# Two of the four weight sums of each seven-product set formed by adding transfers instead of VectorE

## The chip, the cores and the metric

The kernel runs on one core of a Trainium2 chip. TensorE (PE in the profile) multiplies matrices, VectorE (DVE) and ScalarE (ACT) work on elements, GpSimd (POOL) has a small part, and SyncE (SP) issues almost all transfers between the device memory (HBM) and the on-chip memory (SBUF). Each engine takes its instructions in the order in which the program lists them; an engine that waits holds up everything listed behind the wait. The metric is the device time of one execution in microseconds (us). Lower is better.

## The reference

One decoder layer over 512 tokens of width 1024, in float32, batch 1. The two feed-forward blocks, which the change touches, are

```
mod = silu(c) @ w_ada + b_ada                    # nine vectors of 1024: shift, scale, gate, three times
u = rmsnorm(h) * g * (1 + sc) + sh
a, b = split(u @ w_in, 2)                        # w_in: 1024 x 5632, so a and b: 512 x 2816
h = h + 0.5 * gt * ((silu(a) * b) @ w_out)       # w_out: 2816 x 1024
```

The first block runs before, the second after a token-mixing block (a pooling mixer and a dilated window attention, gated and merged), which the change leaves alone. A last RMSNorm ends the layer.

## The kernel before

Activations are kept transposed, features on the 128 partitions and the 512 tokens along the free axis, so each product has a 128x128 block of a weight as the stationary operand and tokens as the moving one. To keep float32 accuracy each operand is split in two parts, hi and lo, and every product is three matmuls: hi*hi, hi*lo, lo*hi.

**The weight stream.** `plan` (L144) writes out by hand one list of *loads* (chunks of at most 128 x 1024 numbers, 512 KB) and one list `order` of *units*, the 128 x 1024 weight pieces in the sequence in which TensorE uses them. For each unit, `split_hi` (L271) has ScalarE copy the piece, rounded, into a ring `whi` (L294), and `split_lo` (L300) has VectorE store the rest into the ring `wlo` (L306). The rings hold about seven units. `look(n)` (L315) is called before each piece of TensorE work; it first lets `fetch` (L215) issue every load for which a buffer is free, then splits units up to n places ahead of the one about to be used (n is 4 around the code that changes, 3 in `ffn_tile`). A buffer comes free when the last unit that reads it has been split, which `self.last` records; the list of free buffers has three entries (`raw`, L1353) and two more (`rawx`, named X in the trace) from the first seven-product set of each feed-forward block on.

**Seven products in place of eight.** Most of `w_in` is used in sets of four column tiles (two gate tiles and two up tiles, `duo`, L723). Rows of `w_in` and tokens are cut in halves, and a two-by-two block product is done with seven block products instead of eight, in Winograd's manner. It needs sums of blocks of u, made once per feed-forward block by `u_steps` (L673), and sums of the weight blocks r11, r12, r22, r21, made for each set. I call one run of `duo` a *set*; there are seven sets in the first feed-forward block and nine in the second. `blocks` (L166) lists a set's seven units, u0 to u6:

```
u0 = r11              u1: x0 = r12 - r11    u2: x1 = r22 - x0    u3 = r21
u4: r12 = r22 - r12   u5 = r22              u6: x0 = r21 - x1
```

The four differences are made by VectorE in `make` (L234, the instruction is L240), each one 128 x 1024 subtraction. A make is issued just ahead of the split of its unit, or right after the ScalarE copy of the unit before it when its load has been issued.

**Around the products.** In `duo` (L754 to L777) each of the seven products is 24 matmuls of 256 columns (`product`, L712, lines L719 to L721). The products accumulate in three PSUM banks A, B, C; their order is A, B, A, C, A, B, A. After product 0 ScalarE copies A to C (`copy(C, A)`, L726 in the trace as bank<-bank), after product 1 B to p5, and so on; the next product on the same bank can't start before the copy has read it. `look(4)` before product 0 lists the split of u4, so the ScalarE copy of u4 stands ahead of `copy(C, A)` in ScalarE's order:

```
self.look(4)
self.product(bank, u, start)
self.step()
if i == 0:
    copy(C, A)
```

**The queue of SyncE.** `fetch` issues loads on SP (L224). In the first feed-forward block the same queue also carries the 512 KB pieces of `w_ada` for the nine vectors (`ada_fetch`, L348, L352), two of them in flight into the buffers `cs` and `AR`. `bg` (L379) has VectorE reduce such a piece (`ada_do`, L355, L360), and then lists the load of the next one into the same buffer, which must wait for that reduction. `ffn_pair` (L662) runs `bg` after each of its two tiles, so between the `look` of its second tile and the `look` before the next set's product 0 there is one such load.

Of the kernel before, what the change touches and what calls it, by code (L numbers as in the profile page):

```python
# [14 lines left out]
P = 128  # L15
# [121 lines left out]
class Kernel:  # L137
# [6 lines left out]
    def plan(self):  # L144
        (i1, o1), mix, (i2, o2) = chunk_widths()
        self.chunks = []
        for name, ws in (("wf1i", i1), ("wf1o", o1), ("wmix", mix), ("wf2i", i2), ("wf2o", o2)):
            off, rec = 0, []
            for w in ws:
                rec.append((name, off, w))  # L150
                off += P * w
            self.chunks.append(rec)
        f1i, f1o, mx, f2i, f2o = self.chunks


        self.loads, self.order, self.last = [], [], {}
        self.shifted = set()

        def plain(recs):
            for r in recs:  # L160
                n = len(self.loads)
                self.loads.append(r)
                self.last[n] = len(self.order)
                self.order.append((r[2], n, ("raw", n), None))

        def blocks(recs):  # L166
            n = len(self.loads)
            self.shifted.update(range(len(self.order), len(self.order) + 7))
            self.loads.extend(recs)
            r11, r12, r22, r21 = (("raw", n + i) for i in range(4))  # L170
            x0, x1 = ("x", 0), ("x", 1)
            for need, src, make in ((0, r11, None), (1, x0, (x0, r12, r11)), (2, x1, (x1, r22, x0)), (3, r21, None),
                                    (3, r12, (r12, r22, r12)), (3, r22, None), (3, x0, (x0, r21, x1))):
                for j, x in enumerate((r11, r12, r22, r21)):
                    if x == src or (make and x in make):
                        self.last[n + j] = len(self.order)
                self.order.append((D, n + need, src, make))

        def shift(i):

            self.shifted.update(range(len(self.order) - i, len(self.order)))

        def ffn(n, ins, outs, first):
            j, at = first, 0
            if first:
                plain(ins[:KT])
                at = KT
            for part, (k0, k1) in enumerate(PARTS):
                while j < pairs_before(n, part):
                    if j < PLAIN[n]:  # L190
                        plain(ins[at:at + 2])
                        if n and j < 2:
                            shift(2)
                        j, at = j + 1, at + 2
                    else:
                        blocks(ins[at:at + 4])
                        j, at = j + 2, at + 4
                plain(outs[part * KT // 2:(part + 1) * KT // 2] if part + 1 < len(PARTS) else outs[-KT:])

        ffn(0, f1i, f1o, FIRST)  # L200
        shift(3)
        base = len(self.order)
        plain(mx)
        self.shifted.update(range(base, base + 4))
        shift(2)
        ffn(2, f2i, f2o, 0)
        shift(4)
        self.fetched = self.done = self.made = 0
        self.pos, self.held, self.retired, self.half = 0, None, [], None
        self.at, self.start, self.top = {}, {}, 0  # L210
        self.buf = {}
        self.units = {base + i: 2 * P for i in (4, 5)}
        self.units.update({base + i: T for i in range(16, 20)})

    def fetch(self, n=None):  # L215

        n = len(self.order) - 1 if n is None else min(n, len(self.order) - 1)
        while self.fetched <= self.order[n][1] and self.free:
            i = self.fetched
            name, off, w = self.loads[i]  # L220
            src = self.a[name][off:off + P * w].rearrange("(p n) -> p n", p=P)
            self.buf[i] = self.free.pop(0)
            for c in self.pieces(i, w):
                self.nc.sync.dma_start(self.buf[i][:, c], src[:, c])  # L224
            self.fetched += 1

    def pieces(self, i, w):
# [6 lines left out]
    def make(self, i):  # L234

        while self.made <= i:
            m = self.order[self.made][3]
            if m:
                out, x, y = (self.source(z) for z in m)
                self.nc.vector.tensor_tensor(out, x, y, op=OP.subtract)  # L240
            self.made += 1

    def unit(self, i):
# [429 lines left out]
    def u_steps(self, n):  # L673
# [18 lines left out]
        def whole(u, k):  # L692
# [2 lines left out]
            return lambda: v.tensor_tensor(u.rearrange("p (k t) -> p k t", k=4), hi, lo, op=OP.add)  # L695

        last = split(3, a12)
        return ([whole(a11, 0), whole(a12, 4)] if n else []) + [add(a22, a21, a22, OP.add), split(0, a22), add(a21, a11, a21, OP.subtract), split(2, a21),
                add(a11, a22, a11, OP.subtract), split(1, a11), add(a12, a12, a11, OP.subtract)], last

    def step(self):

# [20 lines left out]
    def duo(self, j, first, last):  # L723
# [30 lines left out]
        for i, (bank, u, start) in enumerate(((A, blk(lo4, T1), True), (B, S[0], True), (A, S[1], False),  # L754
                                              (C, blk(hi4, T1), False), (A, S[2], False), (B, S[3], False),
                                              (A, blk(hi4, T2), False))):
            if i == 6:
                v.tensor_tensor(q(c)[:, :, 1, :], r(u3), r(p5), op=OP.add)
            self.look(4)
            self.product(bank, u, start)  # L760
            self.step()
# [12 lines left out]
                copy(u3, A)  # L774
            elif i == 6:
                silu(1, A)
                v.tensor_tensor(q(c)[:, :, 0, :], r(B), r(u2), op=OP.add)  # L777
        if last:
            mult()
            high()  # L780
# [783 lines left out]
```

## Time and profile before

| | |
|---|---|
| median of 3 runs | 1017.11 us (1016.72 to 1018.24) |
| span of the profiled execution | 1018.4 us; no other time of that execution is recorded |
| PE busy | 1007.5 us, 99% |
| PE weight loads busy | 913.3 us, 90% |
| DVE busy | 756.1 us, 74% |
| ACT busy | 437.2 us, 43% |
| POOL busy | 26.2 us, 3%, in 30 instructions |
| HBM read | 135.82 MB |
| granted TensorE clock | 0.997 |

A row of the timeline gives the start in us, the duration in us, the engine, the source line, the operation and its operands by tile name, with the idle time before it and what ended that in brackets. SPq rows are transfers being issued; their length is that of the issue, not of the transfer. A busy share of 99% for PE says only that matmuls overlap; whether TensorE really lost time is seen from the distance between its instructions' starts.

### The profile page before, as it was taken

What the parts mean: (1) busy time and instruction counts of PE and PEld (TensorE: products, weight loads), DVE (VectorE), ACT (ScalarE), POOL (GpSimd) and SP (SyncE); (2) the same over time, 40 slices, a digit from 0 to 9 for tenths busy, and PEclk for the clock granted to TensorE, in tenths of its full rate; (3) what the DMA queues carried; (4) which work ended last, traced back from release to release, by engine and by line L of the source; (5) the groups of instructions that cost most, each with busy time, mean ns of one, the idle gap of its engine ahead of it and who ended that gap; (6) DMA issues with size and microseconds to landing.
All of it is one profiled execution on the core that took longest, in us unless ns stands there. A gap on an engine that the chain in (4) does not pass through costs nothing.

```text
span 1018.4 us, 15580 instructions
## 1 busy us (share of the span) xinstructions
PE 1007.5 (99%) x6364; PEld 913.3 (90%) x6364; DVE 756.1 (74%) x1112; ACT 437.2 (43%) x668; POOL 26.2 (3%) x30
## 2 busy tenths in 40 slices
PE   8999999999999999999999999999999999999997
PEld 7888898989999999889988888998899899998997
DVE  6979879889786776879447776577787776676764
ACT  5453352625444552233414323364366254352553
POOL 0000000000000000007100000000000000000001
PEclk9999999999999999999999999999999999999998
DMA  8856465455533413122154773312243234241312
GB/s 314 287 196 246 136 211 176 175 168 174 168 111 112 147 46 104 52 83 83 32 198 167 248 271 121 117 53 78 88 168 123 80 105 145 84 144 44 111 34 83
DMA packets 43114, 139.61 MB, mean 137 GB/s; under 512 B 4897, under 2 KB 8225, under 8 KB 43042
## 3 DMA queue, kind: packets, MB, share of 16 engines
q1 hardware_dynamic: 42354, 137.95, 40.8%
q8 instruction: 50, 0.82, 0.3%
q10 hardware_dynamic: 688, 0.66, 0.2%
q14 instruction: 22, 0.18, 0.1%
HBM read 135.82 MB, written 2.77 MB: 136 GB/s over the span
## 4 chain that ended last, share of the span: by engine, by line
PE 94%; DVE 4%; ACT 0%; issue 0%; DMA 0%; DVEq 0%; ACTq 0%
PE bank L337 17%; PE bank L338 17%; PE bank L339 17%; PE bank L719 10%; PE bank L721 10%; PE bank L720 10%; PE bank L1494 1%; PE bank L1496 1%; PE bank L1498 1%; PE bank L1090 1%; PE bank L1269 1%; PE bank L1423 1%; PE bank L1270 1%; PE bank L1271 1%; PE bank L1038 1%; DVE wlo L306 1%
## 5 line engine op out<-in xcount | busy, mean ns | idle before, releaser
L306 DVE TENSOR_TENSOR wlo<-raw,whi 128x1024 fp32r<-128x1024 f32 (+6 forms) x173 | 177.4, 1037 | 67.6 <-ACT whi L294 67.1
L294 ACT ACTIVATE whi<-raw 128x1024 fp32r<-128x1024 f32 (+6 forms) x173 | 152.3, 899 | 40.6 <-DVE raw L240 39.0
L337 PE MATMUL bank<-UH,whi 128*128 128x512 f32 (+1 forms) x432 | 158.3, 366 | 0.0
L338 PE MATMUL bank<-UL,whi 128*128 128x512 f32 (+1 forms) x432 | 154.2, 357 | 0.1
L339 PE MATMUL bank<-UH,wlo 128*128 128x512 f32 (+1 forms) x432 | 154.1, 357 | 0.0
L337 PE MATMUL bank<-HI,whi 128*128 128x512 f32 (+1 forms) x406 | 146.6, 361 | 0.0
L338 PE MATMUL bank<-HK,whi 128*128 128x512 f32 (+1 forms) x406 | 146.3, 360 | 0.0
L339 PE MATMUL bank<-HI,wlo 128*128 128x512 f32 (+1 forms) x406 | 146.2, 360 | 0.0
L721 PE MATMUL bank<-UH,wlo 128*128 128x256 f32 x512 | 141.6, 277 | 0.0
L719 PE MATMUL bank<-UH,whi 128*128 128x256 f32 x512 | 141.6, 277 | 0.0
L720 PE MATMUL bank<-UL,whi 128*128 128x256 f32 x512 | 141.6, 277 | 0.0
L306 DVE TENSOR_TENSOR wlo<-X,whi 128x1024 fp32r<-128x1024 f32 (+4 forms) x96 | 105.3, 1103 | 39.0 <-ACT whi L294 38.7
L719 PE MATMUL bank<-SH,whi 128*128 128x256 f32 x384 | 107.1, 279 | 0.1
L720 PE MATMUL bank<-SL,whi 128*128 128x256 f32 x384 | 107.0, 279 | 0.0
L721 PE MATMUL bank<-SH,wlo 128*128 128x256 f32 x384 | 106.9, 278 | 0.0
L294 ACT ACTIVATE whi<-X 128x1024 fp32r<-128x1024 f32 (+4 forms) x96 | 89.9, 958 | 32.1 <-DVE X L240 28.9
L720 PEld LDWEIGHTS bank<-UL,whi 128*128 128x128 f32 x512 | 96.3, 188 | 0.3
L719 PEld LDWEIGHTS bank<-UH,whi 128*128 128x128 f32 x512 | 96.1, 188 | 0.3
L721 PEld LDWEIGHTS bank<-UH,wlo 128*128 128x128 f32 x512 | 96.1, 188 | 0.0
L339 PEld LDWEIGHTS bank<-UH,wlo 128*128 128x128 f32 x432 | 81.3, 188 | 12.1
L338 PEld LDWEIGHTS bank<-UL,whi 128*128 128x128 f32 x432 | 81.2, 188 | 11.7 <-issue 0.5
L337 PEld LDWEIGHTS bank<-UH,whi 128*128 128x128 f32 x432 | 81.2, 188 | 11.3 <-issue 0.5
(225 smaller groups left out, 1746.4 us busy)
## 6 DMA issues: line engine op xcount, KB each, us to landing
ada<-wada SPq DMA_DIRECT2D x47, 512.0 KB, 5.0
raw<-wmix SPq DMA_DIRECT2D x44, 512.0 KB, 3.6
raw<-wf1i SPq DMA_DIRECT2D x34, 512.0 KB, 4.3
raw<-wf2i SPq DMA_DIRECT2D x30, 512.0 KB, 3.5
X<-wf2i SPq DMA_DIRECT2D x14, 512.0 KB, 3.6
cs<-wada SPq DMA_DIRECT2D x12, 512.0 KB, 3.5
AR<-wada SPq DMA_DIRECT2D x12, 512.0 KB, 4.0
raw<-wf2o SPq DMA_DIRECT2D x12, 512.0 KB, 3.6
```

Of the source, the lines that this page charges most:

```text
L294: self.nc.scalar.activation(self.hi[:, y], r[:, x], AF.Copy)
L306: self.nc.vector.tensor_tensor(self.lo[:, y], r[:, x], self.hi[:, y], op=OP.subtract)
L337: M(ps, hi, uh, start=start, stop=False)
L338: M(ps, hi, ul, start=False, stop=False)
L339: M(ps, lo, uh, start=False, stop=stop)
L719: M(o, hi, uh, start=start and p == 0 and k == 0, stop=False, skip_group_check=True)
L720: M(o, hi, ul, start=False, stop=False, skip_group_check=True)
L721: M(o, lo, uh, start=False, stop=k == 3, skip_group_check=True)
L1038: M(S[:, o + i * P:o + i * P + P], qz[:, (2 * i + h) * P:(2 * i + h + 1) * P], k[:, toks], start=True, stop=True)
L1090: M(o, pt[:, blk * P:blk * P + P], v, start=i == 0, stop=i == len(srcs) - 1)
L1269: M(b, self.UH[k][:, c::4], hi, start=k == 0, stop=False)
L1270: M(b, self.UH[k][:, c::4], lo, start=False, stop=False)
```

## The change

Each set now has five loads instead of four: w11, t1, w22, w21, t3. For t1 and t3 SP loads the block w12 as before, and then a second transfer, issued on GpSimd's queue with an adding operation, adds another block from HBM onto it in SBUF: t1 = w12 + w11 and t3 = w12 + w22. w12 is thus loaded twice, and w11 and w22 are each read a second time by the adding transfers. The units become

```
u0 = r11   u1 = t1   u2: x1 = t1 + r22   u3 = r21   u4 = t3   u5 = r22   u6: x0 = x1 + r21
```

so `make` has two sums per set left, now additions. Since t1 and x1, t3 and x0 differ in sign from what they replace, two of the sums of u in `u_steps` and the two combining steps of the results in `duo` change between add and subtract; they are the same number of instructions of the same shapes. The adding transfer has to wait until the load under it has landed. The buffers stay the same: three, and five from product 0 of a block's first set on. r11's buffer now comes free after the split of u0, and t1's after the split of u2.

```diff
         def blocks(recs):
             n = len(self.loads)
             self.shifted.update(range(len(self.order), len(self.order) + 7))
-            self.loads.extend(recs)
-            r11, r12, r22, r21 = (("raw", n + i) for i in range(4))
+            w11, w12, w22, w21 = recs
+            self.loads.extend((w11, w12 + w11[:2], w22, w21, w12 + w22[:2]))
+            r11, t1, r22, r21, t3 = (("raw", n + i) for i in range(5))
             x0, x1 = ("x", 0), ("x", 1)
-            for need, src, make in ((0, r11, None), (1, x0, (x0, r12, r11)), (2, x1, (x1, r22, x0)), (3, r21, None),
-                                    (3, r12, (r12, r22, r12)), (3, r22, None), (3, x0, (x0, r21, x1))):
-                for j, x in enumerate((r11, r12, r22, r21)):
+            for need, src, make in ((0, r11, None), (1, t1, None), (2, x1, (x1, t1, r22)), (3, r21, None),
+                                    (4, t3, None), (4, r22, None), (4, x0, (x0, x1, r21))):
+                for j, x in enumerate((r11, t1, r22, r21, t3)):
...
-            name, off, w = self.loads[i]
-            src = self.a[name][off:off + P * w].rearrange("(p n) -> p n", p=P)
+            name, off, w, *more = self.loads[i]
+            at = lambda name, off: self.a[name][off:off + P * w].rearrange("(p n) -> p n", p=P)
             self.buf[i] = self.free.pop(0)
             for c in self.pieces(i, w):
-                self.nc.sync.dma_start(self.buf[i][:, c], src[:, c])
+                self.nc.sync.dma_start(self.buf[i][:, c], at(name, off)[:, c])
+            if more:
+                self.nc.gpsimd.dma_start(self.buf[i], at(*more), accum_op=OP.add)
...
-                self.nc.vector.tensor_tensor(out, x, y, op=OP.subtract)
+                self.nc.vector.tensor_tensor(out, x, y, op=OP.add)
...
-        return ([whole(a11, 0), whole(a12, 4)] if n else []) + [add(a22, a21, a22, OP.add), split(0, a22), add(a21, a11, a21, OP.subtract), split(2, a21),
-                add(a11, a22, a11, OP.subtract), split(1, a11), add(a12, a12, a11, OP.subtract)], last
+        return ([whole(a11, 0), whole(a12, 4)] if n else []) + [add(a22, a21, a22, OP.subtract), split(0, a22), add(a21, a11, a21, OP.subtract), split(2, a21),
+                add(a11, a22, a11, OP.subtract), split(1, a11), add(a12, a12, a11, OP.add)], last
...
-                v.tensor_tensor(q(c)[:, :, 1, :], r(u3), r(p5), op=OP.add)
+                v.tensor_tensor(q(c)[:, :, 1, :], r(p5), r(u3), op=OP.subtract)
...
-                v.tensor_tensor(q(c)[:, :, 0, :], r(B), r(u2), op=OP.add)
+                v.tensor_tensor(q(c)[:, :, 0, :], r(B), r(u2), op=OP.subtract)
```

## The prediction

> **What bounds the kernel now.** I read the page's busy times and its chain of waits first, then the table of stretches over the sets, then the timeline of each engine at the first set of a block.
>
> ```profile
> PE 1007.5 (99%) x6364; PEld 913.3 (90%) x6364; DVE 756.1 (74%) x1112; ACT 437.2 (43%) x668; POOL 26.2 (3%) x30
> ...
> PE 94%; DVE 4%; ACT 0%; issue 0%; DMA 0%; DVEq 0%; ACTq 0%
> ...
> 128.50:147.72 19.22, 19.22 (x169) 19.21 (x167) 15.68 (x17) 12.40 (x16) 0.00 (x0) 1.00 0.64 229
> 169.62:208.03 38.41, 38.41 (x337) 38.41 (x335) 33.06 (x36) 21.10 (x28) 0.00 (x0) 1.00 0.56 185
> 229.93:268.68 38.75, 38.70 (x336) 38.50 (x335) 34.42 (x41) 21.11 (x28) 0.00 (x0) 1.00 0.57 184
> 290.58:329.00 38.42, 38.42 (x337) 38.42 (x336) 27.86 (x29) 19.43 (x27) 0.00 (x0) 1.00 0.35 113
> sum 307.66, PE 307.61 PEld 307.38 DVE 239.53 ACT 165.68 POOL 0.00; mean PE 38.45 PEld 38.42 DVE 29.94 ACT 20.71 POOL 0.00
> ```
>
> TensorE holds 94% of the chain. The table's stretches are runs of sets; the columns are PE, PEld, DVE, ACT and POOL busy, then the granted clock, the DMA share and GB/s. The sum row covers all eight runs, sixteen sets: 307.66 us. One set takes 19.22 us, two take 38.42, whether DVE is busy 33.06 us of them or 27.86. The only run that is longer is the one from 229.93: 38.75 instead of 38.42, so 0.33 us lost. That is all that the sixteen sets lose to anything but TensorE's own pace, and it bounds what relief of DVE can bring there.
>
> **What is removed.** The next row is the table for L240 alone, over the whole span; below it is the chain inside the stretch where DVE falls behind.
>
> ```profile
> 0.00:1018.40 1018.40, 78.05 (x64) 1.00 0.41 137
> ...
> 213.80 1.22 DVE cs L360 x2
> ...
> 231.07 1.14 DVE X L240
> ...
> 238.49 1.15 DVE X L240
> 239.79 0.90 issue
> 240.69 0.58 ACT u L726
> 241.31 0.39 PE bank L719
> ```
>
> The 64 makes cost DVE 78.05 us; half go, so 39 us, all beside matmuls. From 213 to 240 us the chain runs through DVE, which has the `w_ada` reductions to do as well, and ends in the 0.33 us gap at 241.31. The make at 231.07 is u4's and goes (1.14 us); the one at 238.49 is u6's and stays. 1.14 is more than 0.33, so the gap closes: **-0.33 us**. What is late next there is TensorE itself. The changed signs are as many instructions of the same shapes: 0.
>
> **What is added.** Per set one more load on SP and two adding transfers on POOL's queue, 3 x 512 KB, for sixteen sets 25 MB on top of 135.8 MB. POOL has 0.00 us of work in the sets, so its queue is empty; the DMA share there is 0.34 to 0.64, and 7 transfers in 19.22 us instead of 4 fit if they are in time. So the cost is not volume but lateness: t1 and t3 are ready only after two transfers, one behind the other. I call A the time from the landing of the load under it to the landing of the adding transfer. The trace has no such transfer. Its nearest rows (KB each, median us from issue to landing), and the one measured duration of a POOL instruction that I use:
>
> ```profile
> raw<-wf1i SPq DMA_DIRECT2D x34, 512.0 KB, 4.3
> raw<-wf2i SPq DMA_DIRECT2D x30, 512.0 KB, 3.5
> ...
> scr<-q SPq DMA_DIRECT2D x1, 528.0 KB, 2.6
> v<-scr SPq DMA_DIRECT2D x1, 528.0 KB, 3.8
> ...
> L1157 POOL TENSOR_SCALAR k<-rt 64x496 f32<-64x496 f32 x4 | 6.0, 1510 | 0.3
> ```
>
> An adding transfer must fetch a block from HBM, read the block in SBUF and write it. From below, it is one plain load: A = 3.5. From above, two of the slower ones: A = 8.6, and 10.1 with a POOL instruction of 1.51 us ahead. I take the two streams that it is made of, one out of SBUF (2.6) and one into it (3.8): **A = 6.4**, an estimate that lies between the ends.
>
> The Trainium skill, DMA: Bandwidth & Descriptors, section Anatomy of one DMA — SWDGE (gpsimd) path, fits a transfer issued from GpSimd as 2.0 us plus its bytes at 436 GB/s, an estimate of 3.2 us for 512 KB, or 4.4 if the bytes count twice; with these the sum below would be 1019.3 or 1020.5. No run here shows a transfer of that queue yet.
>
> **Place 1: the first set of the first block.** Only three buffers exist before its product 0. By the code t3, the fifth load, takes t1's buffer, which is given back at the split of u2; the next `look` is the one before product 0. On SP that is behind the `w_ada` load that `bg` lists after the pair's second tile.
>
> ```profile
> 128.50 0.28 PE L719 MATMUL bank<-UH,whi 128*128 128x256 f32 x1
> ...
> 131.33 0.28 PE L719 MATMUL bank<-SH,whi 128*128 128x256 f32 x1
> ...
> 134.21 0.28 PE L719 MATMUL bank<-SH,whi 128*128 128x256 f32 x1
> ...
> 129.96 1.05 ACT L294 ACTIVATE whi<-raw 128x1024 fp32r<-128x1024 f32 x1
> 132.01 1.07 ACT L294 ACTIVATE whi<-raw 128x1024 fp32r<-128x1024 f32 x1 [1.00 <-DVE raw L240]
> 132.97 0.58 ACT L726 ACTIVATE bank<-bank 128x512 f32<-128x512 f32 x1
> ...
> 120.95 1.28 DVE L306 TENSOR_TENSOR wlo<-X,whi 128x256 fp32r<-128x256 f32 x2
> 124.84 1.23 DVE L306 TENSOR_TENSOR wlo<-X,whi 128x1024 fp32r<-128x1024 f32 x1 [1.46 <-ACT whi L294]
> 125.98 1.22 DVE L360 SCALAR_TENSOR_TENSOR AR<-AR,cond 128x1024 f32<-128x1024 f32 x1
> ...
> 123.41 0.33 SPq L352 DMA_DIRECT2D cs<-wada  x1
> 123.83 0.38 SPq L224 DMA_DIRECT2D raw<-wf1i  x1
> 127.24 0.33 SPq L352 DMA_DIRECT2D AR<-wada  x1
> ```
>
> Products 0, 1 and 2 start at 128.50, 131.33 and 134.21. u4's ScalarE copy runs at 132.01, behind its make; copy(C, A) follows and ends at 132.97 + 0.58 = 133.55. Product 2 adds to bank A and needs that copy, so u4's copy may start no later than 134.21 - (133.55 - 132.01) = 132.67. There is 0.66 us of room today.
>
> After: the `AR` load still goes out at 127.24, for it waits for the reduction at 125.98, which no removed make delays (the split ahead of it, at 124.84, waited 1.46 us for ACT). t3's load follows 0.42 later, as the load at 123.83 follows the one at 123.41: 127.66. It takes 4.3, lands at 131.96, and the sum is there at 131.96 + A. ACT stands at u4's copy until then, with copy(C, A) behind it, and TensorE at product 2. The stall is 131.96 + A - 132.67 = A - 0.71: **5.69 us** for 6.4. It is paid once: behind it ACT has 3.7 us of copies (three of 1.05, one of 0.58) for the 5.7 us until product 4 wants the next one, and DVE's split of u4, 1.22 us after ACT's, is wanted only two products later. u4's own make, which DVE drops, was not what TensorE waited for.
>
> **Place 2: the first set of the second block.** The same three buffers, no `w_ada` loads, but t3's buffer waits for t1 as a sum.
>
> ```profile
> 734.94 0.28 PE L719 MATMUL bank<-UH,whi 128*128 128x256 f32 x1
> ...
> 731.70 1.06 ACT L294 ACTIVATE whi<-raw 128x1024 fp32r<-128x1024 f32 x1 [5.00 <-DVE raw L240]
> 737.97 0.58 ACT L726 ACTIVATE bank<-bank 128x512 f32<-128x512 f32 x1 [5.20 <-PE bank L721]
> ...
> 715.23 0.33 SPq L224 DMA_DIRECT2D raw<-wf2i  x1
> ...
> DMA to landing us min/median/max: 4.4/4.4/4.4
> ```
>
> u4's copy runs at 731.70 and then ACT idles 5.20 us, so there is room. The deadline, by the spacings of place 1, is 734.94 + 5.71 - 1.54 = 739.11. t1 is the second load, issued at 715.23 and landing 4.4 later (the last row is that load's), at 719.6; as a sum at 719.6 + A. ACT's copy (1.05) and DVE's two reads of it (1.22 each, the first beside the copy) hold the buffer about 2.4 more; t3's load lands 3.5 later and is a sum A later: 725.5 + 2A. The stall is 2A - 13.6 where that is positive: 0 for 6.4 (12.8), hidden by 0.8 us; the cover is gone at A = 6.8.
>
> **The other fourteen sets** have five buffers. The tightest are the eight sets that follow another set directly, where t3 takes the buffer of the r21 before it.
>
> ```profile
> 760.71 0.33 SPq L224 DMA_DIRECT2D X<-wf2i  x1
> 761.09 0.42 SPq L224 DMA_DIRECT2D raw<-wf2o  x1
> ...
> DMA to landing us min/median/max: 3.5/3.5/4.5
> ...
> 776.39 0.58 ACT L726 ACTIVATE bank<-bank 128x512 f32<-128x512 f32 x1 [1.17 <-PE bank L721]
> ```
>
> t3's load would go where the one at 761.09 stands, behind r21's at 760.71; the slowest there took 4.5, so it lands at 765.6. The next set's copy(C, A) is at 776.39 and must end 2.88 us after product 0, near 779.2, so u4's copy may start at 777.6. Hidden up to A = 12. t1 has 7 units' time and is no tighter. Sets behind output tiles have more, since those units last twice as long. SP's order else only shifts by one load per set.
>
> **The sum**, against the span of 1018.4: + 5.69 + 0 - 0.33 = +5.4, so 1023.8. The median of the runs lies 1.3 under that span, so for the median 1017.1 + 5.4 = **1022.5**.
>
> **The rivals.**
> *The adding transfer is as short as a plain one* (A = 3.5): 2.79 - 0.33 = +2.5, 1019.6. For it: a 528 KB transfer out of SBUF lands in 2.6. Against: it has both to read and to write SBUF. The Trainium skill's fit named above would be this case.
> *It is long* (A from 6.8 to 12): both first sets stall. At 8.6: 7.89 + 3.6 - 0.33 = +11.2, 1028.3; at 10.1: 9.39 + 6.6 - 0.33 = +15.7, 1032.8. For it: nothing in the trace prices POOL's part of the issue.
> *It is so long that the steady sets stall* (A above 12). At 15: 14.3 + 16.4 + 8 x 3 - 0.33 = +54, 1071. Against: more than three times any 512 KB row.
> *Not slower: t3 is in time.* t1's buffer is physically free when DVE's split of u1 has read it, near 122.2 (the row at 120.95). If t3's load stood on SP before 122.0, not behind the `AR` load, it would land at 126.3 and be a sum by 132.7, and the stall at place 1 would vanish: -0.33, 1016.8. Against it is the order of the code: nothing fetches between the split of u2 and the `look` before product 0.
> *Faster by more than can be told apart*, if 39 us less DVE work helps TensorE in a way that the 0.33 us don't show. Nothing in the set table speaks for it: two sets with 5.2 us more DVE work than two others (33.06 and 27.86) last as long.
>
> **How the numbers follow.** Chances: place 1 alone with A from 4.4 to 6.8, 45%; short, 19%; long, 17%; steady sets stall, 6%; in time, 9%; faster, 4%. The time is that of the first. A median of these runs can be told from another at about 0.2%, 2.0 us. Slower then holds the first four but a hundredth of the short case, 86%; same 10%; faster 4%. The range runs from 1018.8 (A near 2.8) to 1032.7 (A = 10.1) and leaves out the steady stall, the in-time and the faster case and the edge of the short one, 2 in 10.
>
> **What the profile after would show.** 32 instructions at L240 and about 39 us less DVE; POOL's queue with 32 transfers; in the sets' table 38.4 for all pairs but a first set of 19.2 + 5.7 in the first block, with ACT's copy of u4 idle on a DMA just before copy(C, A), and t3's load issued just behind an `AR` load. The second block's first run stays at 57.6. I am wrong if the first set stays at 19.2 (the in-time rival), if the eight following sets grow, or if matmuls of the same shape are spaced differently.

## The result, and the profile after

The changed kernel takes 1042.92 us (median of 4 runs, 1040.52 to 1043.74), the kernel before on the same chip 1017.67 us (4 runs, 1016.72 to 1019.89). The ratio is 1.0241 with a 95% interval of 1.0221 to 1.0261. The forecast was 1022.5 us with a range up to 1032.7: the sign was right, the added time was nearly five times what was forecast. The profiled execution of the changed kernel took 1043.39 us, with a span of 1041.6 us.

From the page of the kernel after: busy times, the two large transfer queues, what was read, and the chain of waits by engine.

```profile
PE 1010.3 (97%) x6364; PEld 914.2 (88%) x6364; DVE 720.3 (69%) x1080; ACT 437.4 (42%) x668; POOL 54.3 (5%) x62
...
q1 hardware_dynamic: 44658, 146.34, 41.2%
q0 software_dynamic: 4608, 16.78, 9.2%
...
HBM read 160.98 MB, written 2.77 MB: 157 GB/s over the span
...
PE 80%; DMA 9%; DVE 6%; ACT 2%; issue 2%; SPq 0%; DVEq 0%; ACTq 0%; POOLq 0%
```

32 VectorE instructions and 35.8 us of VectorE work are gone, and 32 transfers stand on GpSimd's queue (q0). TensorE's share of the chain falls from 94% to 80%, and transfers, which held nothing, hold 9%.

The table of stretches of the kernel after, one row for each run of sets, from its first matmul to the first one behind it. The columns are PE, PEld, DVE, ACT and POOL busy, the granted clock, the DMA share and GB/s.

```profile
125.65:152.53 26.88, 21.74 (x170) 21.52 (x168) 14.71 (x15) 12.26 (x16) 1.73 (x2) 0.87 0.64 200
174.31:217.77 43.46, 39.36 (x337) 38.76 (x336) 31.60 (x37) 19.75 (x26) 2.60 (x3) 1.00 0.73 212
239.56:282.10 42.54, 39.73 (x337) 39.27 (x336) 31.84 (x38) 19.84 (x27) 2.36 (x3) 1.00 0.72 217
303.89:342.42 38.53, 38.53 (x338) 38.53 (x337) 25.13 (x27) 19.11 (x26) 0.86 (x1) 1.00 0.49 148
747.65:815.68 68.03, 60.05 (x505) 59.64 (x504) 42.30 (x43) 33.11 (x44) 5.20 (x6) 0.95 0.62 175
837.47:876.00 38.53, 38.53 (x338) 38.53 (x337) 25.68 (x26) 20.05 (x27) 1.74 (x2) 1.00 0.54 159
897.78:936.31 38.53, 38.53 (x338) 38.53 (x336) 25.68 (x26) 20.03 (x27) 1.74 (x2) 1.00 0.55 159
958.09:996.62 38.53, 38.53 (x337) 38.52 (x336) 24.61 (x26) 19.19 (x27) 0.88 (x1) 1.00 0.44 137
sum 335.03, PE 315.01 PEld 313.31 DVE 221.57 ACT 163.34 POOL 17.12; mean PE 39.38 PEld 39.16 DVE 27.70 ACT 20.42 POOL 2.14
```

With the same borders, the runs of the kernel before took 19.33, 38.52, 38.87, 38.53, 57.73, 38.53, 38.52 and 38.53 us, 308.56 in all. So the sets lost 26.5 us, in four runs of the eight: 7.5 in the first set, 4.9 and 3.7 in the next two runs, 10.3 in the second block's first run. 20.0 us of it are idle time of TensorE (335.03 - 315.01); the other 6.5 are matmuls that took longer. The stretches between the runs are as before, but for the start: the sets begin at 125.65 us instead of 128.50. That is no effect of the change: among the kernels below one without any adding transfer starts its sets at 125.69 (e5_dose), one with all of them at 128.74 (e4_early_fetch). It goes with the TensorE clock at the start. The trace before records full clock from 19.27 us on, e4_early_fetch from 19.86, the kernel after from 11.57 and e5_dose from 11.66; around 12 us eight matmuls of 128x1 take 1.71 us in the first two and 0.99 and 1.03 in the others. 26.5 less these 2.9 and 0.4 in stretches elsewhere is the 23.2 us between the two spans.

**Where it waits.** Rows of the timeline of the kernel after, queue by queue: first at the first set of the first block, then at the second run of sets, then in the second block's first run. Brackets give the idle time before the row and what ended it.

```profile
124.39 0.33 SPq L355 DMA_DIRECT2D AR<-wada  x1
124.81 0.38 SPq L225 DMA_DIRECT2D raw<-wf1i  x1
...
129.75 0.86 POOL L227 DMA_DIRECT2D raw<-wf1i  x1 [21.93 <-DVE wlo L309]
...
135.07 1.06 ACT L297 ACTIVATE whi<-raw 128x1024 fp32r<-128x1024 f32 x1 [6.91 <-DMA raw<-wf1i]
136.03 0.58 ACT L729 ACTIVATE bank<-bank 128x512 f32<-128x512 f32 x1
...
136.66 0.58 PE L722 MATMUL bank<-SH,whi 128*128 128x256 f32 x1 [5.14 <-ACT bank L729]
...
176.27 0.33 SPq L355 DMA_DIRECT2D AR<-wada  x1
176.70 0.37 SPq L225 DMA_DIRECT2D raw<-wf1i  x1
...
183.43 0.88 POOL L227 DMA_DIRECT2D raw<-wf1i  x1 [22.09 <-DMA raw<-wf1i]
...
192.50 1.06 ACT L297 ACTIVATE whi<-raw 128x1024 fp32r<-128x1024 f32 x1 [4.76 <-DMA raw<-wf1i]
193.46 0.58 ACT L729 ACTIVATE u<-bank 128x512 f32<-128x512 f32 x1
...
194.10 0.39 PE L722 MATMUL bank<-UH,whi 128*128 128x256 f32 x1 [2.01 <-ACT u L729]
...
757.31 0.81 SPq L225 DMA_DIRECT2D X<-wf2i  x2
...
763.03 0.86 POOL L227 DMA_DIRECT2D X<-wf2i  x1 [14.14 <-DMA X<-wf2i]
...
771.07 1.06 ACT L297 ACTIVATE whi<-X 128x1024 fp32r<-128x1024 f32 x1 [9.59 <-DMA X<-wf2i]
...
772.66 0.58 PE L722 MATMUL bank<-UH,whi 128*128 128x256 f32 x1 [6.45 <-ACT u L729]
```

The first place is the one forecast, link by link: t3's load 0.42 us behind the `AR` load, the adding transfer behind the landing of that load, ScalarE idle on it, copy(C, A) behind u4's copy, and TensorE idle for 5.14 us. The other two were not forecast. There it is t1 that is late, the second unit of a set that directly follows another. ScalarE reaches that unit while TensorE is still in the set ahead, and stands at it with the copy of bank A (L729, at 193.46) behind it; so the matmul that waits is the first of the last product of the set ahead. The adding transfer is issued at 183.43 and ScalarE starts on the sum at 192.50, 9.07 us later; at 763.03 and 771.07 it is 8.04 us. The first set of the second block lost 1.53 us on its own t3 (matmul at 755.05).

**The transfers.** The table for the adding line, L227, over the whole execution: durations of the issuing instruction (min/median/max in ns; one of four such rows), and the time from issue to landing of all 32.

```profile
L227 POOL DMA_DIRECT2D raw<-wf2i x12: 858/872/917, 733.1 to 970.2; - x12
...
DMA to landing us min/median/max: 5.1/6.7/9.2
```

**The clock.** Stretches of the kernel after around the first long stall; the column before the last two is the granted clock.

```profile
131.10:136.50 5.40, 0.42 (x4) 0.21 (x2) 0.34 (x1) 1.43 (x2) 0.00 (x0) 0.81 0.55 97
136.60:138.60 2.00, 1.94 (x9) 1.94 (x10) 1.77 (x2) 2.00 (x4) 0.00 (x0) 0.50 0.08 14
138.60:140.60 2.00, 2.00 (x11) 2.00 (x11) 2.00 (x3) 1.00 (x2) 0.00 (x0) 0.50 0.89 264
140.60:142.60 2.00, 2.00 (x17) 2.00 (x16) 1.72 (x2) 1.16 (x3) 0.00 (x0) 0.83 0.91 285
```

The clock falls to half while TensorE waits, and stays there for 6.83 us in the records, so the product behind the stall runs at half speed: 11 matmuls in 2 us in place of 17 and more. The first set lost 7.5 us: 5.3 is the delay at the stall (5.42 us from one matmul start to the next, where 0.12 is usual), the other 2.2 is this. The same happens behind the stall at 772.66.

### The profile page after: what moved, and what is told of

It is laid out like the page before. It is cut to its first block, busy times and chain, and to the rows that moved or that the text cites. A ratio compares the mean times of both kernels' runs of the same rounds, so it can differ in the third digit from the quotient of the medians.

```text
span 1041.6 us, 15684 instructions
## 1 busy us (share of the span) xinstructions
PE 1010.3 (97%) x6364; PEld 914.2 (88%) x6364; DVE 720.3 (69%) x1080; ACT 437.4 (42%) x668; POOL 54.3 (5%) x62
## 3 DMA queue, kind: packets, MB, share of 16 engines
q0 software_dynamic: 4608, 16.78, 9.2%
## 4 chain that ended last, share of the span: by engine, by line
PE 80%; DMA 9%; DVE 6%; ACT 2%; issue 2%; SPq 0%; DVEq 0%; ACTq 0%; POOLq 0%
PE bank L340 15%; PE bank L341 15%; PE bank L342 15%; PE bank L722 8%; PE bank L724 8%; PE bank L723 8%; DMA X<-wf1i 3%; DMA AR<-wada 2%; DVE wlo L309 2%; DMA raw<-wf2i 2%; PE bank L1497 1%; PE bank L1501 1%; PE bank L1499 1%; DMA X<-wf2i 1%; PE bank L1093 1%
## 5 line engine op out<-in xcount | busy, mean ns | idle before, releaser
L309 DVE TENSOR_TENSOR wlo<-raw,whi 128x1024 fp32r<-128x1024 f32 (+5 forms) x182 | 190.4, 1058 | 85.6 <-ACT whi L297 83.5
L297 ACT ACTIVATE whi<-raw 128x1024 fp32r<-128x1024 f32 (+5 forms) x182 | 163.8, 917 | 55.8 <-DMA raw<-wf1i 33.4
L309 DVE TENSOR_TENSOR wlo<-X,whi 128x1024 fp32r<-128x1024 f32 (+4 forms) x87 | 92.0, 1067 | 56.8 <-ACT whi L297 56.7
L297 ACT ACTIVATE whi<-X 128x1024 fp32r<-128x1024 f32 (+4 forms) x87 | 78.8, 928 | 36.4 <-DMA X<-wf1i 14.3
```

Of the source, the lines that this page charges most:

```text
L297: self.nc.scalar.activation(self.hi[:, y], r[:, x], AF.Copy)
L309: self.nc.vector.tensor_tensor(self.lo[:, y], r[:, x], self.hi[:, y], op=OP.subtract)
```

## The experiments

Times are medians of 4 runs (10 for e1_no_add and e7_hybrid), with the kernel before on the same chip: 1017.33 us beside e1 to e4 (but e3b), 1017.62 beside e5, e6, e7 and e10, 1017.01 beside e11 to e13, and 1017.35 beside e3b. A set's length is taken as in the table above, from the one profiled execution of each kernel. That is not always a typical one: those of e2_plain_pool and e3b_t1_only were the fastest of their four, 2.9 and 1.8 us under the median. A stall is given as the idle time before its row; where an expectation speaks of a hold, its number is the distance between two matmul starts, which is 0.28 us longer. Where an edit adds a line, the line numbers of its rows are one higher.

**No adding transfer (e1_no_add).** The kernel after without them; SP's five loads, the order and VectorE's two sums stay. t1 and t3 are then w12 alone, so all sums by transfer are left out.

```diff
-            if more:
-                self.nc.gpsimd.dma_start(self.buf[i], at(*more), accum_op=OP.add)
```

> The changed kernel without the 32 adding transfers (t1 and t3 are then w12 alone, so the sums are left out); the fifth load of each set, the new order of buffers and the two makes per set stay. Theory 1, the loss is the wait for sums that are late in a few sets: all sets run at 19.2 us and the time is that of before, 1016 to 1018. Rival, the fifth load and the changed order of buffers cost by themselves: 1025 or more stays.

Measured: 1017.15 us (1016.12 to 1020.03), ratio 1.0004 [0.9993, 1.0016]. All runs of sets are back at 19.33, 38.53 and 57.73 us, but the third, which took 39.18. So the loss needs the second transfers: the fifth load, SP's new order and the changed signs cost nothing but perhaps those 0.3 us, and 36 us less VectorE work bring nothing.

**The second transfer without the addition (e2_plain_pool).** It is issued on GpSimd's queue, with the same bytes, the same wait and the same place, but overwrites; so w12's part of the sums is left out.

```diff
-                self.nc.gpsimd.dma_start(self.buf[i], at(*more), accum_op=OP.add)
+                self.nc.gpsimd.dma_start(self.buf[i], at(*more))
```

> The second transfer of t1 and t3 is plain instead of adding, still on GpSimd's queue and still behind the landing of the load under it (the sums are left out). Theory 1a, half of the length of an adding transfer is the adding itself (its 4 KB packets take 328 ns, those of plain loads 159): the second transfer lands 1.6 to 3 us sooner, the first set stalls some 3.7 us instead of 5.3, runs two and three of the first block lose 2 us or less in place of 8.6, the second block's first run 3 to 4 in place of 10.3; about 1026. Rival 1b, two transfers in a row and GpSimd's way of issuing are the length: 1038 or more.

Measured: 1031.06 us (1028.2 to 1031.58), ratio 1.0131 [1.0116, 1.0147], between the two. The first set takes 24.97 us (5.6 more) and the second block's first run 62.85 (5.1 more), both with half clock for 3.41 us; the second and third run of the first block take 38.53, no loss at all. Landing takes 3.7/4.5/6.8 us (min/median/max) in place of 5.1/6.7/9.2. From the page of this kernel, the row of GpSimd's queue:

```profile
q0 software_dynamic: 4608, 16.78, 5.0%
```

As many packets and bytes as in the kernel after took 5.0% of 16 engines' span instead of 9.2%. Per packet that is 16 x 0.050 x 1026.4 / 4608 = 0.18 us, against 16 x 0.092 x 1041.6 / 4608 = 0.33: the addition nearly doubles the time that a packet holds a DMA engine. By the medians, 13.7 of the 25.3 us are the second transfer as such, behind the first, and the rest is the addition's; in the two profiled executions it is 10.4 of 26.5 in the sets.

**Only t3, only t1 (e3_t3_only, e3b_t1_only).** In the first, t1's adding transfers are left out (t1 = w12), in the second t3's.

```diff
-            self.loads.extend((w11, w12 + w11[:2], w22, w21, w12 + w22[:2]))
+            self.loads.extend((w11, w12, w22, w21, w12 + w22[:2]))
```
```diff
+            self.loads.extend((w11, w12 + w11[:2], w22, w21, w12))
```

> Adding transfers for t3 alone; t1 is w12 alone (its sum is left out). Theory 1 as read from the trace: t3 stalls the first set of the first block (5.3 us and 2.2 more at half clock, 7.5), t1 stalls runs two and three of that block (8.6) and the second set of the second block (6.6 and 1.8), and it makes t3 late in that block's first set (1.7). So 7.5 stay and the time is about 1025. Rival, t3 is the late one in runs two and three too: 1033 or more.

> The other half of the run with t3's sums alone: the sixteen adding transfers of t1 stay, those of t3 are left out, so that sum is missing in every set. If t1 is what holds the second and third run of the first block and the first run of the second (4.9, 3.7 and 10.3 us), and t3 what holds the first set, the first set is 19.3 us again, the three runs keep most of their 18.9 us, and the time is 1030 to 1036 us. Rival: t1 is late there only because both transfers of a set stand on GpSimd's queue and share the DMA engines; then the three runs lose most of what they lost, and the time is below 1026 us.

Measured: with t3 alone 1025.99 us (1024.48 to 1027.8), ratio 1.0093 [1.0076, 1.011]; with t1 alone 1023.15 us (1021.32 to 1024.02), ratio 1.0052 [1.0032, 1.0073]. The one run of sets that is longer with t3 alone, and then the one that clearly is with t1 alone, from the tables of stretches:

```profile
125.83:152.90 27.07, 21.78 (x170) 21.57 (x168) 14.71 (x15) 12.26 (x16) 1.00 (x1) 0.87 0.64 202
```
```profile
732.36:793.61 61.25, 58.22 (x505) 58.02 (x504) 41.76 (x43) 32.64 (x44) 2.58 (x3) 1.00 0.56 169
752.20:754.20 2.00, 2.00 (x17) 2.00 (x18) 1.84 (x2) 1.81 (x2) 0.00 (x0) 1.00 0.09 31
```

t3 alone costs the first set 7.7 us, and nothing in any other: all of place 1, and t3's transfers of the fifteen other sets are hidden, as forecast. t1 alone costs 3.5 us in the second block and 0.1 in the first. Together they make 11 us in the profiled sets, not 26.5 (by the medians 8.7 + 5.8 = 14.5, not 25.3). The second and third run of the first block lose only when both transfers are there, so the first account of e3b, that t1 by itself holds them, fell and its rival held. (The last row is the clock behind a stall of 3.03 us: full.)

**Loads listed earlier (e4_early_fetch).** `look` fetches once more after its splits, so that t3's load stands on SP ahead of the `w_ada` load. Nothing is left out.

```diff
         self.fetch()
         self.split(self.pos + ahead)
+        self.fetch()
```

> The changed kernel, complete, with one line more: look() issues loads again right after its splits, so that a load is listed on SP as soon as its buffer is given back and not behind the w_ada loads that come before the next look(). Theory 2, in the first block the place on SP behind w_ada loads makes the sums late: the first set's 7.5 and most of the 8.6 of runs two and three go, the second block keeps its 10.3; 1026 to 1029. Rival, the length of the adding transfer alone decides: 1038 or more.

Measured: 1041.1 us (1038.39 to 1044.52), ratio 1.0238 [1.0214, 1.0261]. The first set is nearly cured (21.12 us, 1.8 more, at full clock), so place 1 is the order on SP. The second and third run are no better, 43.79 and 46.58 us, so for them theory 2 fell. Rows of the second run: GpSimd's, SP's queue, then VectorE's.

```profile
172.18 0.87 POOL L227 DMA_DIRECT2D raw<-wf1i  x1 [13.60 <-DMA raw<-wf1i]
...
172.94 0.33 SPq L356 DMA_DIRECT2D AR<-wada  x1
...
180.89 1.22 DVE L364 SCALAR_TENSOR_TENSOR AR<-AR,cond 128x1024 f32<-128x1024 f32 x1 [4.37 <-DMA AR<-wada]
182.04 0.08 DVE L364 DVE_READ_ACCUMULATOR AR<-AR,cond 128x1 f32 x1
182.04 1.29 DVE L309 TENSOR_TENSOR wlo<-raw,whi 128x256 fp32r<-128x256 f32 x2
```

t1's adding transfer now goes out at 172.18, half a microsecond into the run and not nine as in the kernel after, and the `w_ada` load at 172.94 runs beside it: it lands at 180.86, after 7.9 us. VectorE stands at that piece's reduction for 4.37 us with the splits and makes of the set behind it. The wait has moved from t1 to the load beside its transfer.

**Without the `w_ada` loads, and both edits together (e6_no_ada_loads, e10_early_no_ada).** In the first block's sets the loads into `cs` and `AR` are left out after the first two; the second kernel has the earlier listing too.

```diff
-        for c in np.split(np.arange(D), n):
+        self.ring = getattr(self, "ring", 0) + (self.ada_free is not None)
+        for c in np.split(np.arange(D), n) if self.ring < 3 or self.ada_free is None else ():
```

> The changed kernel without the w_ada loads of the first block's sets, after the first two; the reductions stay and read old data, so that part of the computation is left out. Theory L (the second and third run of sets of the first block lose their 4.9 and 3.7 us to the w_ada loads, which stand on SP ahead of the load of the sums and share the transfers with it): both runs go back to 38.5 us, the first set keeps a part of its loss or none, the second block keeps its 10 us, and the time is 1027 to 1035 us. Rival (the sums themselves take too long there, or VectorE's reductions are what holds them): the two runs keep their losses and the time is about 1042 us.

> The last edit and the earlier listing of the loads together. If the losses of the first block are the listing (first set) and the w_ada loads (second and third run), nothing but the second block's 10 us and at most 2 us of the first set are left: 1027 to 1030 us. If the sums of the second and third run are late for another reason, their 5 and 8 us stay: about 1041 us.

Measured: 1025.68 us (1024.78 to 1027.68), ratio 1.0063 [1.0045, 1.008]; with both 1027.92 us (1026.39 to 1028.1), ratio 1.0079 [1.0064, 1.0094]. The first block loses nothing in the first kernel (19.32, 38.53, 38.53 and 38.53 us) and 0.4 in the second; the second block keeps 9.0 and 10.1. The second and third run without these loads:

```profile
166.10:204.63 38.53, 38.53 (x338) 38.53 (x336) 29.66 (x32) 20.31 (x26) 1.73 (x2) 1.00 0.56 158
226.41:264.94 38.53, 38.53 (x337) 38.52 (x336) 30.91 (x37) 19.95 (x27) 1.73 (x2) 1.00 0.54 156
```

So all 16 us of the first block hang on the `w_ada` loads, beside which the sums are made. The edit takes away their bytes and their places on SP together.

**Small `w_ada` loads (e13_small_ada).** This tells their bytes from their place: they stay on SP, but load 128 of 1024 columns.

```diff
-            c = slice(c[0], c[-1] + 1)
+            c = slice(c[0], c[-1] + 1 if self.ring < 3 or self.ada_free is None else c[0] + 128)
```

> The changed kernel with the w_ada loads of the first block's sets cut to their first 128 columns (an eighth of the bytes) after the first two, in the same places of SP's list, with whole reductions that read old data behind them; so part of that computation is left out. Theory O (the loss of the first block comes from the order on SP, where the load of a sum waits behind a w_ada load and through it for VectorE): the first block keeps most of its 16 us, and the time stays at 1037 us or more. Theory S (the loss comes from the transfers that w_ada's loads and the adding ones share, which makes both late): the first block loses what it lost without these loads, and the time is near 1026 us. In between, 1030 to 1036 us, both have a part.

Measured: 1034.88 us (1032.91 to 1035.87), ratio 1.0173 [1.0158, 1.0188]: both have a part, and the sets show which. The first three runs of sets, and then the landing times of the adding transfers in the first block, from 120 to 300 us (min/median/max):

```profile
127.07:153.15 26.08, 21.64 (x170) 21.43 (x168) 14.71 (x15) 12.27 (x16) 1.72 (x2) 0.93 0.64 197
174.93:213.46 38.53, 38.53 (x337) 38.52 (x336) 29.74 (x32) 20.09 (x26) 2.60 (x3) 1.00 0.68 192
235.25:274.40 39.15, 38.77 (x337) 38.57 (x336) 30.89 (x37) 19.97 (x27) 2.60 (x3) 1.00 0.64 189
```
```profile
DMA to landing us min/median/max: 5.2/6.1/9.1
```

The same answer for the kernel after:

```profile
DMA to landing us min/median/max: 5.2/8.0/9.2
```

The first set keeps 6.7 us of its loss: it is the order, and the size of the load ahead matters little. The second and third run lose 0 and 0.3: there it is the bytes. `w_ada` loads of an eighth bring the median landing from 8.0 to 6.1 us and t1 in time. In the second run t1 is ready 10.3 us after the run's start instead of 18.2: its adding transfer lands after 6.1 us instead of 9.05, its plain load after 3.45 instead of 6.4, and that load is issued 1.9 us sooner, behind an `AR` load that also goes out sooner. With the earlier listing, which cured the first set and not the second run, this separates the two causes.

**One sum less in the second block (e12_one_sum_less).** The adding transfer of t1 in its second set is left out.

```diff
-            self.loads.extend((w11, w12 + w11[:2], w22, w21, w12 + w22[:2]))
+            self.sets = getattr(self, "sets", 0) + 1
+            self.loads.extend((w11, w12 + w11[:2] if self.sets != 9 else w12, w22, w21, w12 + w22[:2]))
```

> The changed kernel with one adding transfer left out, that of the second product's sum in the second set of the second block; its plain load stays, so that one sum of one set is missing. If that one transfer holds the first run of the second block (6.7 us of hold and 1.75 us at half clock), the run of 68.0 us falls to about 59.5 us and the time to 1034.4 us; what is left is the hold of the first set's last sum. If the loss only moves to the next sum (the third product's, or the seventh's), the time stays within 2 us of 1042.9 us.

Measured: 1036.88 us (1032.22 to 1041.85), ratio 1.02 [1.0157, 1.0243]; the runs differ too much for the median to decide. In the profiled one that run of sets takes 61.30 us instead of 68.03, no half clock, and a new stall of 2.15 us comes later, ended by ScalarE's copy of t3:

```profile
773.30 1.06 ACT L298 ACTIVATE whi<-raw 128x1024 fp32r<-128x1024 f32 x1 [5.50 <-DMA raw<-wf2i]
```

So some 6.7 of the 10.3 us hang on that one transfer, and 2 us turned into a wait for the next sum. The size is rough: the same execution lost only 2.4 us each in the second and third run of the first block, which the edit leaves alone, instead of 4.9 and 3.7. t1 of this set can't start earlier, since its buffer is among those that appear only behind product 0 of the first set (the load goes out at 757.31, just behind the VectorE split of a sum of u, ending at 757.23, that is the last to read the buffer). More buffers ahead of that weren't tried.

**Stalls without transfers (e5_dose, e11_four_holds).** The kernel before, with ScalarE copies that nothing reads put ahead of copy(C, A): first 11 and 5 of them in the first set of the first and of the fourth run, then 8, 13, 9 and 11 in the first set of each of the four. Nothing is left out.

```diff
             if i == 0:
+                for _ in range({(0, 8): 11, (0, 18): 5}.get((self.blk, j), 0)):
+                    copy(self.tp.tile([P, T], F32, name="ut"), self.cond[:, :T])
                 copy(C, A)
```

> The kernel before, no adding transfer at all; extra ScalarE copies (nothing reads them) are put ahead of the copy that the second product of a set waits for: eleven in the first set of the first block, five in the first set of that block's last run of sets. From 0.58 us a copy they should hold TensorE for some 5.2 us and some 2.3 us. Theory C (the slow products behind a long wait are what the wait itself costs, whatever made it): the granted clock falls to half after the long hold, the first set grows by about 7.5 us, the set with the short hold by 2.3 us only, and the time is about 1027 us. Rival (the slow clock comes from the adding transfers, not from the idle time): no half clock behind either hold, the sets grow by 5.2 and 2.3 us, and the time is about 1025 us.

> The kernel before with extra ScalarE copies as in the first dose, now in the first set of each of the first block's four runs of sets: 8, 13, 9 and 11 copies. By 0.52 us from copy to copy, the 5.23 us hold of the eleven in the first set, and the later runs' cover (five copies there were hidden whole), TensorE is held for about 3.7, 4.2, 2.1 and 3.1 us. If an idle TensorE loses its clock from some length on, some of these holds show half clock and cost 1.5 to 2.5 us more than they last and the shorter ones do not; if it takes a hold as long as 5 us, none does and the time is about 1030 us; with two halvings it is about 1034 us.

Measured: 1024.55 us (1024.25 to 1025.02), ratio 1.0049 [1.0034, 1.0064]; and 1035.79 us (1033.4 to 1037.01), ratio 1.0181 [1.0166, 1.0197]. In the first, eleven copies idle TensorE for 4.95 us, and the set takes 26.81 us, 7.5 more, with half clock for 6.83 us: the loss of the changed kernel's first set, to 0.1 us, without a single adding transfer. (The five copies were hidden whole, which makes the total 2.4 us less than theory C said.) In the second, the stalls are 3.39, 3.82, 2.79 and 0.71 us, and the sets grow by 5.27, 6.98, 4.3 and 1.0. The third stall, then stretches of 2 us behind the second, third and fourth:

```profile
248.70 0.39 PE L719 MATMUL bank<-SH,whi 128*128 128x256 f32 x1 [2.79 <-ACT bank L726]
...
182.90:184.90 2.00, 2.00 (x11) 2.00 (x11) 1.30 (x2) 1.89 (x3) 0.00 (x0) 0.50 0.34 139
...
248.80:250.80 2.00, 2.00 (x10) 2.00 (x11) 2.00 (x2) 2.00 (x3) 0.00 (x0) 0.54 0.89 260
311.70:313.70 2.00, 2.00 (x18) 2.00 (x19) 1.14 (x1) 2.00 (x3) 0.00 (x0) 1.00 0.03 8
```

Over all kernels here, stalls up to 2.15 us left the clock alone; those of 2.79 (e11_four_holds) and 3.12 (e4_early_fetch) halved it, the one of 3.03 between them (e3b_t1_only) didn't; from 3.30 us on all did. Half clock lasted 3.41 us or 6.83, once or twice the same time, and cost 1.4 to 3.0 us beside the delay itself.

The clock records of the traces show why the length of a stall alone doesn't decide. Within one trace all changes of the clock lie whole multiples of 3.413 us apart (in the kernel after at 134.45, 141.27, 769.33 and 776.15 us: 2, 184 and 2 of them from each to the next). These points cut the time into pieces of 3.413 us. In all traces, from the first set to the end of the last, half clock followed each piece at full clock in which TensorE idled for 2.06 us or more (17 pieces), and none in which it idled for 1.93 or less. The stall of 2.79 us lay within one piece; that of 3.03 was cut into 1.93 and 1.10. A piece at half clock was followed by another one where TensorE idled in it for 1.76 us or more (10 pieces), and by full clock where it idled for 0.57 or less. Among the small matmuls at the start of the program half clock came with less idle time (0.11 us in the piece ahead of it in e10_early_no_ada), so idle time is not all that counts. The rule is read from the traces, not tested by a run made for it. The Trainium skill, TensorE: Matmul & The Clock Gate, section Part 1: The HAM clock gate, says that the array falls to half rate after an idle window of about 3.4 us, and that this window of 3413 ns is free-running and not reset by a kernel's start. The spacing of the changes agrees; but the window need not be idle throughout, since 2.06 us of it were enough here.

**Adding transfers where they lost nothing (e7_hybrid).** VectorE's sums in the first five sets of the first block and the first two of the second, adding transfers in the nine others (the expectation counts eight sets and 16 units of VectorE work; it is nine and 18). Nothing is left out.

```diff
-                        blocks(ins[at:at + 4])
+                        blocks(ins[at:at + 4], j < (18, 0, 8)[n])
...
+            if vec:
+                self.loads.extend(recs)
+                r11, r12, r22, r21 = rs = [("raw", n + i) for i in range(4)]
+                us = ((0, r11, None), (1, x0, (x0, r12, r11)), (2, x1, (x1, r22, x0)), (3, r21, None),
+                      (3, r12, (r12, r22, r12)), (3, r22, None), (3, x0, (x0, r21, x1)))
```

> Adding transfers only in the sets that lost nothing (the first block's last two sets, the second block's last six), VectorE's sums as before in the first five sets of the first block and the first two of the second; nothing is left out. If the losses lie only where the sums come late, all sets are as before and the time is 1016.5 to 1018.5 us, with 16 units of VectorE work fewer and nothing gained. Rival (each adding transfer costs something of its own, or the lightened VectorE gives something back): outside that range, by up to 2.3 us below if TensorE's start is the earlier one.

Measured: 1018.19 us (10 runs, 1016.88 to 1020.97), ratio 1.0004 [0.999, 1.0018]. From the table of stretches over its eight runs of sets:

```profile
sum 308.57, PE 308.52 PEld 308.30 DVE 227.21 ACT 165.36 POOL 8.86; mean PE 38.56 PEld 38.54 DVE 28.40 ACT 20.67 POOL 1.11
```

308.57 us against 308.56 before: adding transfers that are in time cost nothing, and the VectorE work that they save is worth nothing. No version here beats the kernel before.

## Why the prediction was wrong

- **What is removed** held. 32 makes went, and with them 35.8 us of DVE's busy time instead of 39; they are worth nothing that can be measured (e1_no_add, e7_hybrid). Whether the 0.33 us gap closes can't be told: the third run took 38.53 us in the kernels with t3 alone and with the plain transfer, but 39.18 without adding transfers.
- **A = 6.4 us**, one size for all places, was mis-sized. From the load's landing it was 5.8 at place 1, where little else is in flight, and 9.4 for the t1 of the second run, where plain loads run beside it; two of those, issued at 183.62 and 186.28, took 8.7 and 8.5 us to land themselves. The bounds, 3.5 to 10.1, held at the places that stalled. The Trainium skill's fit for such a transfer (DMA: Bandwidth & Descriptors, Anatomy of one DMA), an estimate of 3.2 us for 512 KB, is below the shortest plain one here (3.7, of which the issuing instruction is 0.53) and far below the adding ones (5.1 at least).
- **Place 1** held in mechanism and form: A - 0.71 with the measured 5.8 is 5.1, and TensorE idled 5.14. That the stall came so near to the forecast 5.69 is in part luck, since the 6.4 was added up from two unlike transfers. What failed is "It is paid once": the half clock behind it costs 2.2 us more. e5_dose shows that as the price of the idle time itself.
- **Place 2** held in form. With the two measured A, 8.6 for t1 and 6.3 for t3, it gives 14.9 - 13.6 = 1.3; the stall was 1.53. The zero was the mis-sized A.
- **The other fourteen sets** is the step that failed: the sum has nothing for them, and they cost 17.2 us. Its part on t3 is right where t3's transfers stand alone (e3_t3_only). "t1 has 7 units' time and is no tighter" was wrong in three of them, the second sets of three runs. In the second block's second set, t1's load can't be issued before product 0 of the set ahead, as the buffers aren't free until then, so "have five buffers" comes too late for it; that costs 8.6 us with the half clock. In the second and third run of the first block, the `w_ada` loads share the DMA engines with two adding transfers per set and both sums come late, t1 first and t3 of the same set behind it (stalls of 2.01 and 1.37 us in the second run); that costs 8.6 us (e13_small_ada, e6_no_ada_loads). "SP's order else only shifts by one load per set" is true of the order (e1_no_add), and misses that transfers in flight slow each other.
- "So the cost is not volume but lateness" was thus half right. The lateness of t1 in the first block *is* made of volume, in a run whose DMA share was 0.56 before and 0.73 after, on average.
- The first set at 24.9 us was measured at 26.9, the second block's first run at 68.0 instead of 57.6. Of the signs named for a wrong forecast one came true, matmuls of the same shape spaced differently, behind stalls, and a second for three of the eight following sets, whose sums came late.

In numbers: forecast 5.7 at place 1; measured 7.5 there, 8.6 in the first block's next two runs, 1.7 in the second block's first set and 8.6 in its second, 26.5 us in all, of which 6.5 are slower matmuls.

What stays open is how a transfer is slowed by its neighbours. That adding packets hold a DMA engine longer is shown (0.33 against 0.18 us); that this alone makes a plain load beside them take 8 us is not. The Trainium skill, DMA: Bandwidth & Descriptors, section Issuing engines are not separate DMA queues, has all issuing engines share the same 16 DMA engines, which agrees with the `w_ada` load of 7.9 us here. Open too is what more buffers in the second block would save.

## What to carry to other kernels

Work moved off an engine with idle time gained nothing here (36 us of VectorE's); what it is moved onto must be asked for its latency at each place where buffers are few, not for its volume on average. A transfer that waits for another is as late as the two together, and both grew when other loads ran beside them (in the second run the load from 3.45 to 6.4 us and the adding one from 6.1 to 9.05, by the bytes of the `w_ada` loads), so the deadline has to be worked out for every consumer with the slow landing time, not the median. A stall of TensorE of some 3 us or more is to be priced with about 2 us more (1.4 to 3.0 here) for the half clock behind it.

## What was not expected of the hardware

An adding transfer of 512 KB took 5.1 to 9.2 us from GpSimd's issue, whose instruction alone takes 0.87 us; a plain one on the same queue 3.7 to 6.8. Its packets hold a DMA engine 1.8 times as long. A plain load beside it landed after 7.9 us where the medians before were 3.5 to 4.3. TensorE's clock halved at stalls of 2.79 us and 3.12 and all longer ones but not at 3.03, for 3.41 or 6.83 us, and always at points of a grid of 3.413 us; behind the stall of 2.79 us that was 0.25 us after TensorE had started again.
